# x by channels with two chunks on raw x, host-laid bias tables, attention as three chains, and another order of the output projection

## The chip, the cores and the metric

One NeuronCore of a Trainium2 chip runs the whole program. The time is device microseconds of one execution, the median of several. Engines by the profile's names: PE (TensorE matmuls and transposes), DVE (VectorE), ACT (ScalarE), POOL (GpSimd), SP (SyncE, which issues most DMAs).

## The reference

```python
hn = rms_norm(x, ln_g)                      # x: 1024 tokens x 1024 channels, fp32
proj = hn @ w_in + b_in                     # 3584 columns
glu_a, glu_b, z_conv, q, k, v, z_att = split(proj)          # 512 columns each
y_conv = conformer_conv(glu_a, glu_b, ...)  # GLU, 31 depthwise taps, LayerNorm, silu, pointwise 512x512
y_att = neighbourhood_attention(q, k, v, rpb)  # 8 heads of 64, 16x64 grid, window 8x16, bias per head
y_conv = grouped_rms_norm(y_conv) * silu(z_conv)
y_att  = grouped_rms_norm(y_att)  * silu(z_att)
out = rms_norm(x + concat(y_conv, y_att) @ w_out) * final_g
```

## The kernel before

Every fp32 product is made of three fp32r matmuls, hi·hi, lo·hi and hi·lo: an operand's rounded copy (hi) is made by ACT, what the rounding left (lo) by DVE or POOL as source minus hi. All of `mm` stands on line 127, all transposes on 131, all ACT copies on 136, all DVE work on 140, POOL's on 144; so rows are read by tile names.

A planner in Python writes the order of the five engines when the program is built. `Clock.weave` runs generators ("streams") by rank, lets `Ring`s hand out buffers and PSUM banks, keeps estimated queues for ACT, DVE and POOL, and puts the conv taps (`all_taps`) where DVE's queue is short. The engines then run exactly that order.

- **Head.** Eight 512 KB loads bring x by tokens. Per token tile: squares with a sum (ACT, or DVE for tiles 4 and 6), rsqrt as a power on POOL, x times rsqrt (DVE). 64 PE transposes `px` turn it to channels on partitions; ACT makes hi from the bank (times ln_g), DVE lo. From these 16 tiles `hi0..7`, `lo0..7` (128 channels x 1024 tokens, two halves of 512) all projections are computed.
- **Projections.** w_in goes through in 28 chunks of 128 columns: `pb`, `pa` (GLU), `pq`, `pk`, `pv`, `pz` (gates), each 2 halves x 8 k x 3 matmuls of 512 columns. The raw chunk comes by DMA (`wr`), ACT makes `wh`, POOL `wl` (two subtracts of 128x512 a chunk). LEAD and FILL list the chunks' order. `pv` reads hi and lo in a permuted column order.
- **Convolution.** `glu` on DVE, then 31 taps a channel block on `acc` (DVE, 128x1024 each), then per token tile LayerNorm (transposes `ln`, ACT and DVE, transposes back `lnb`), swish (`th`, `uh`, `ul`), the pointwise matmuls `pw`, group norm, transposes `yt`, copies into `acc`.
- **Attention.** 8 heads x 4 column blocks. Scores `s` on PE, bias and row minimum in one DVE operation, exp on ACT (`prob`), transposes `ptp`, hi (`pth`, ACT) and lo (`ptl`, DVE), then `po`. It is one stream: scores(n+1), transposes(n), products(n). The bias tables with -1e30 outside the window are built by the kernel through DRAM (`rp8`, `ab`, `abn`, `row` DMAs) and loaded by four DMAs a table and head (`load_bias`).
- **Gates and end.** `gated` reads a gate's bank after the normalised output y is there. `final_gates` computes `pz11` and `pz27`, then the output projection: w_out split into `woh`, `wol`, y split into `yh`, `yl` per token tile, 17 groups of 24 matmuls of up to 512 columns, residual, final RMSNorm, store. k order 0, 1, 2, 4, 5, 6, 3, 7 (0 to 3 conv, 4 to 7 attention), tiles 0 and 1 interleaved first.

Of the kernel before, what the change touches and what calls it, by code (L numbers as in the profile page):

```python
# [17 lines left out]
P = 128  # L18
# [9 lines left out]
KH = 8  # L28
TAPS = 31
EPS = 1e-6  # L30
NEG = -1e30

# [7 lines left out]
HF = [(0, 11), (4, 12)]  # L40

LEAD = "g0 g1 g2 q0 k0".split()
FILL = "g3 q1 k1 q2 k2 q3 a0 k3 a1 a2 c0 c1 c2".split()
N_PW = 16
# [5 lines left out]
BV = "pj"  # L50
PEL, PEA, PEB, MMO = 0.3, 0.15, 0.15, 0.0025
# [3 lines left out]
QI = 0.1  # L55
LW = 10.9
SQ_DVE = (4,6)
# [32 lines left out]
class Clock:  # L90
# [58 lines left out]
def block(ctx: ExitStack, tc: tile.TileContext, x, vecs, w_in, dw_w, pw_w, pw_b, rpb, w_out, final_g, out):  # L149
# [16 lines left out]
    r_u, r_raw, r_w, r_x, r_uh, r_ul, r_gz, r_y = ring(16), ring(1), ring(2), ring(XB), ring(1), ring(0), ring(1), ring(1)  # L166
    r_pt, r_os = ring(2), ring(2)
# [20 lines left out]

    x2 = x[0]
# [31 lines left out]
    for t in range(4):  # L221
        xload(t)
    raw0 = wraw(0)
    for t in range(4, NT):
        xload(t)
    land = [4.5, 5.9, 7.4, 8.9, 11.8, 13.3, 14.7, 16.2]
    land_w = LW

    vec = half_tile("uh", "vec")[:V_N, :P]
    nc.scalar.dma_start(out=vec, in_=vecs)  # L230
    dwr = half_tile("ul", "dwr")[:TAPS, :C]
    nc.sync.dma_start(out=dwr, in_=dw_w[0])
# [3 lines left out]
    cols = const.tile([P, V_N], F32, name="cols")  # L236
    pv = bank("tr", "pv")
    nc.tensor.transpose(out=pv[:, :V_N], in_=vec, identity=ident[:V_N, :V_N])
    nc.vector.tensor_copy(out=cols, in_=pv[:, :V_N])
# [4 lines left out]
    dwc = const.tile([P, NC4, 32], F32, name="dwc")  # L244

    def tap_cols():
        yield 19.0
        yield from r_tr.get()
        pd = bank("tr", "pd")
        for c in range(NC4):  # L250
            ck.tp(pd[:, c * 32:c * 32 + TAPS], dwr[:, c * P:(c + 1) * P], ident[:TAPS, :TAPS])
        t = ck.dve("tensor_scalar", out=dwc[:, :, :TAPS],
                   in0=pd[:, :NC4 * 32].rearrange("p (c k) -> p c k", k=32)[:, :, :TAPS], scalar1=0.5, scalar2=None,
                   op0=ALU.mult)
        r_tr.put(t)
        r_ul.put(t)
# [4 lines left out]
    x_ready, hn_ready = {}, {}  # L261

    def x_tile(t):
        yield land[t]
        ss = sm.tile([P, 1], F32, tag="ss", name=f"ss{t}")
        rs = sm.tile([P, 1], F32, tag="rs", name=f"rs{t}")
        eng = "dve" if t in SQ_DVE else "act"
        while t >= 4 and ck.q[eng] > ck.now + QI:
            yield ck.now + 0.1
        if t in SQ_DVE:  # L270
            e = ck.dve("scalar_tensor_tensor", out=acc[:, t % 4, :], in0=xt[t], scalar=1.0 / 1024.0, in1=xt[t],
                       op0=ALU.mult, op1=ALU.mult, accum_out=ss)
        else:
            e = ck.act(out=acc[:, t % 4, :], in_=xt[t], func=AF.Square, scale=1.0 / 32.0, accum_out=ss)
        yield e
        ck.gps("tensor_scalar", 0.2, e, out=rs, in0=ss, scalar1=EPS, scalar2=None, op0=ALU.add)
        e = ck.gps("tensor_tensor", 0.47, 0.0, out=rs, in0=rs, in1=mhalf[:, :1], op=ALU.pow)
        yield e
        x_ready[t] = ck.dve("tensor_scalar", e, 0.55, out=xt[t], in0=xt[t], scalar1=rs, scalar2=None, op0=ALU.mult)

    def turned(h):

        todo_ = list(range(NK))
        for group in ((("tr", "tr", "s", "s", "o", "ln"),) if h == 0 else ()) + (("tr",), ("s",)) * NK:
            ks, todo_ = todo_[:len(group)], todo_[len(group):]
            pts = []
            for k, tag in zip(ks, group):
                yield from RB[tag].get()
                pts.append((k, tag, bank(tag, f"px{h}_{k}", NB[tag])))
            for j in range(4):  # L290
                t = 4 * h + j
                while t not in x_ready:
                    yield ck.now + 0.1
                if x_ready[t] + ck.HOP > ck.now:
                    yield x_ready[t] + ck.HOP
                for k, tag, pt in pts:
                    ck.tp(pt[:, j * P:(j + 1) * P], xt[t][:, k * P:(k + 1) * P], ident)
                    if j == 3:
                        sl = slice(512 * h, 512 * h + 512)
                        e = ck.act(out=hi[k][:, sl], in_=pt, func=AF.Copy, scale=col(V_LN + k))  # L300
                        ck.spawn(low(h, k, pt, sl, e, RB[tag]), -1)
            yield
        for _ in range(4):
            r_u.put()

    def all_turned():
        for h in range(2):
            yield from turned(h)

    def low(h, k, pt, sl, t, r):  # L310
        yield t
        t = ck.dve("scalar_tensor_tensor", t, out=lo[k][:, sl], in0=pt, scalar=col(V_LN + k),
                   in1=hi[k][:, sl].bitcast(F32), op0=ALU.mult, op1=ALU.subtract)
# [12 lines left out]
    ck.q["pool"] = 5.0
# [10 lines left out]
    def prefetch():  # L337
        for n in range(len(order)):
            if n < W_AHEAD or "pw" in state:
                yield from r_raw.get()  # L340
                raw, end = (wraw(n), ck.now + 4.0) if n else (raw0, land_w)
# [7 lines left out]
            for k0 in range(0, NK, KS):  # L349
                kk = slice(k0, k0 + KS)  # L350
                t = ck.act(out=whi[:, kk, :], in_=raw[:, kk, :], func=AF.Copy)
                ck.jobs.append((t, partial(low_weight, n, raw, whi, wlo, kk)))
                yield

    def low_weight(n, raw, whi, wlo, kk):
        k = dict(out=wlo[:, kk, :], in0=raw[:, kk, :], in1=whi[:, kk, :].bitcast(F32), op=ALU.subtract)
        t = ck.gps("tensor_tensor", 0.1 + 0.0022 * KS * P, **k)
        ready.setdefault(n, (whi, wlo, []))[2].extend([t] * KS)
        if kk.stop == NK:
            r_raw.put(t)  # L360
# [875 lines left out]
```

## Time and profile before

| | us |
|---|---|
| median of 3 runs (lowest, highest) | 569.93 (569.51, 573.39) |
| the profiled execution | 572.21 |
| its span, first to last instruction | 570.4 |
| PE busy | 539.3 |
| DVE busy | 412.2 |
| ACT busy | 260.1 |
| POOL busy | 195.1 |

The profiled execution is 1.81 us longer than its span, and 2.28 above the median. Busy times of PE count pipelined matmuls, whose durations overlap; what one matmul adds to the time is read from a run of equal ones.

### The profile page before, as it was taken

The page shows a single profiled execution, that of the slowest core. Times are in us where ns is not written, and L with a number is a line of the kernel's source. Part 1 is how long each engine was busy: PE and PEld are TensorE (multiplying, and loading weights), DVE is VectorE, ACT ScalarE, POOL GpSimd, SP SyncE. Part 2 cuts the span into 40 slices and gives each one's busy share as a digit, 9 for nine tenths or more (in the row PEclk, how much of TensorE's full clock was granted, in tenths as well). Part 3 has the DMA queues.
Part 4 walks back from the last instruction along what each step waited for, and adds up shares of the span by engine and source line. Part 5 has one row for each costly group of instructions (what it writes and reads, how often), then busy time and mean ns, then how long its engine had stood idle before and what let it go on. Part 6 is the DMA issues. An engine that isn't in the chain of part 4 may idle for free.

```text
span 570.4 us, 7827 instructions
## 1 busy us (share of the span) xinstructions
PE 539.3 (95%) x2717; PEld 447.2 (78%) x2717; DVE 412.2 (72%) x665; ACT 260.1 (46%) x634; POOL 195.1 (34%) x176
## 2 busy tenths in 40 slices
PE   4999999898999998999997999999999999999995
PEld 3688888676888886888786788788888888888885
DVE  4747999987999979988999884667564365464232
ACT  6552221124555153655465645875665555253121
POOL 7513543232222343232525152542515552031121
PEclk9999999998999999999998999999999999999999
DMA  9413546663123442263241241101101470044221
GB/s 330 145 14 84 168 128 223 172 192 111 40 57 103 125 105 66 74 149 103 65 142 54 77 120 46 38 26 52 39 0 38 158 284 0 2 148 145 78 75 74
DMA packets 62331, 57.74 MB, mean 101 GB/s; under 512 B 9981, under 2 KB 51765, under 8 KB 62292
## 3 DMA queue, kind: packets, MB, share of 16 engines
q1 hardware_dynamic: 62222, 57.22, 33.6%
q8 instruction: 21, 0.34, 0.3%
q14 instruction: 18, 0.15, 0.1%
q10 hardware_dynamic: 70, 0.03, 0.0%
HBM read 36.58 MB, written 11.58 MB: 84 GB/s over the span
## 4 chain that ended last, share of the span: by engine, by line
PE 71%; DVE 17%; DMA 4%; issue 3%; ACT 2%; SPq 2%; POOL 1%; POOLq 0%; ACTq 0%; DVEq 0%
PE out L127 15%; PE pz L127 13%; DVE acc L140 12%; PE pv L127 6%; PE pk L127 6%; PE pq L127 5%; PE po L127 4%; PE pw L127 4%; PE pb L127 4%; PE ptp L131 3%; PE pa L127 3%; PE s L127 3%; DMA kl<-kl 1%; PE po L131 1%; DMA x<-in_x 1%
## 5 line engine op out<-in xcount | busy, mean ns | idle before, releaser
L140 DVE SCALAR_TENSOR_TENSOR acc<-glu,dwc,acc 128x512 f32<-128x512 f32 (+25 forms) x150 | 186.7, 1270 | 1.2
L144 POOL TENSOR_TENSOR wl<-wr,wh 128x512 fp32r<-128x512 f32 x56 | 93.9, 1695 | 153.0 <-ACT wh L136 147.7
L127 PE MATMUL pz<-hi,wh 128*128 128x512 f32 x128 | 52.2, 408 | 0.0
L127 PE MATMUL out<-wol,yh 128*128 128x512 f32 (+1 forms) x136 | 51.2, 377 | 0.0
L127 PE MATMUL out<-woh,yl 128*128 128x512 f32 (+1 forms) x136 | 51.2, 377 | 0.0
L127 PE MATMUL out<-woh,yh 128*128 128x512 f32 (+1 forms) x136 | 51.2, 377 | 0.0
L127 PE MATMUL pz<-hi,wl 128*128 128x512 f32 x128 | 50.3, 393 | 0.1
L127 PE MATMUL pz<-lo,wh 128*128 128x512 f32 x128 | 50.1, 391 | 0.0
L136 ACT ACTIVATE wh<-wr 128x512 fp32r<-128x512 f32 x56 | 32.3, 628 | 30.5 <-DMA wr<-in_w_in 20.9
L140 DVE TENSOR_TENSOR ptl<-ptp,pth 128x512 fp32r<-128x512 f32 x64 | 37.0, 614 | 1.2 <-ACT pth L136 1.2
L136 ACT ACTIVATE pth<-ptp 128x512 fp32r<-128x512 f32 x64 | 31.8, 543 | 13.2 <-PE ptp L131 12.4
L140 DVE CUSTOM_DVE_ANT_0 s<-s,bias 128x264 f32<-128x264 f32 (+1 forms) x64 | 30.2, 512 | 7.3 <-PE s L127 4.2
L140 DVE TENSOR_TENSOR xr<-out,xr 128x512 f32<-128x512 f32 (+1 forms) x17 | 11.1, 660 | 33.6 <-PE out L127 29.1
L136 ACT ACTIVATE prob<-s,mx 128x264 f32<-128x264 f32 (+1 forms) x64 | 33.6, 536 | 0.6 <-DVE mx L140 0.4
L136 ACT ACTIVATE os<-po 128x256 f32<-128x256 f32 x32 | 12.4, 387 | 41.9 <-PE po L127 41.8
L131 PE MATMUL ptp<-ident,prob 128*128 128x128 f32 x224 | 30.0, 273 | 0.0
L127 PE MATMUL pq<-hi,wh 128*128 128x512 f32 x64 | 26.6, 416 | 3.2 <-DVE v L140 3.2
L127 PE MATMUL po<-pth,v 128*128 128x256 f32 x112 | 29.5, 291 | 0.0
L144 POOL TENSOR_TENSOR ams<-ams,mhalf 128x8 f32<-128x8 f32 x8 | 14.6, 1819 | 43.5 <-DVE ams L140 43.5
L127 PE MATMUL po<-ptl,v 128*128 128x256 f32 x112 | 29.3, 290 | 0.0
L127 PEld LDWEIGHTS out<-woh,yh 128*128 128x128 f32 x136 | 25.6, 188 | 4.7
L127 PEld LDWEIGHTS out<-woh,yl 128*128 128x128 f32 x136 | 25.6, 188 | 4.7
(153 smaller groups left out, 1371.0 us busy)
## 6 DMA issues: line engine op xcount, KB each, us to landing
wr<-in_w_in SPq DMA_DIRECT2D x28, 512.0 KB
x<-in_x SPq DMA_DIRECT2D x8, 512.0 KB
wor<-in_w_out SPq DMA_DIRECT2D x8, 512.0 KB
xr<-in_x SPq DMA_DIRECT2D x8, 512.0 KB
out<-xr SPq DMA_DIRECT2D x16, 256.0 KB
kh<-kh SPq DMA_DIRECT2D x24, 128.0 KB
kl<-kl SPq DMA_DIRECT2D x24, 128.0 KB
q<-ql SPq DMA_DIRECT2D x16, 128.0 KB
```

The source lines that it names most:

```text
L127: self.nc.tensor.matmul(out, lhsT=lhsT, rhs=rhs, start=start, stop=stop)
L131: self.nc.tensor.transpose(out=out, in_=in_, identity=identity)
L136: self.nc.scalar.activation(**k)
L140: getattr(self.nc.vector, fn)(**k)
L144: getattr(self.nc.gpsimd, fn)(**k)
```

## The change

The host now hands over x a second time by channels (`xt`), w_in with each chunk contiguous, taps and vectors as columns, and three finished bias tables; q's weights and bias are scaled by 0.125 in the kernel instead of the scores (their low part is made on DVE).

- **Head.** x comes by channels in 16 half rows of 256 KB. The first two chunks (`RAW`: pb0, pa0) are multiplied with raw x times ln_g, and their results by `rsb` (the rsqrt of each token, on all partitions) afterwards. Per half row: hi copy and square on ACT, lo on DVE, the squares' sum on DVE. `stats`: 4 transposes `sq`, 4 ACT copies with sums, the power on POOL, 4 more transposes that broadcast, one ACT copy. Then `normalise`: xc times ln_g times rsb (DVE), hi again (ACT), lo again on DVE (even k) or POOL (odd k). Only then can the chunks after the second run.
- **Attention.** Three streams: `all_scores`, `turns`, `attention`, with two sets of `prob`. The v transposes `pvt` use the banks o and ln instead of pj; `pv` reads hi and lo in plain order.
- **Gates.** z = (pz + b)(1 + tanh) of the conv gates goes to a kept tile before y is ready (3 DVE operations, before 2). FILL has a0 and a1 earlier; N_PW is 20. The planner's costs for PE and DVE are raised.
- **End.** k order 4 to 7, then 0 to 3. The first group is tiles 0, 1 and 2, its PSUM banks s, s, pj, pj, o, tr. The last two of w_out's splits (k = 2, 3) take tiles that come free after pw7. x is loaded again after all splits.

```diff
+RAW = ((0, 0), (1, 0))
-FILL = "g3 q1 k1 q2 k2 q3 a0 k3 a1 a2 c0 c1 c2".split()
-N_PW = 16
+FILL = "g3 q1 k1 a0 q2 k2 a1 q3 k3 a2 c0 c1 c2".split()
+N_PW = 20
...
+    def x_raw(k, h):
...
+        t = ck.act(out=hi[k][:, sl], in_=xc[k][:, sl], func=AF.Copy, scale=col(V_LN + k))
...
+        t2 = ck.act(out=sq, in_=xc[k][:, sl], func=AF.Square, scale=1.0 / 32.0)
+        yield t
+        raw_ready[k, h] = ck.dve("scalar_tensor_tensor", t, out=lo[k][:, sl], in0=xc[k][:, sl], scalar=col(V_LN + k),
+                                 in1=hi[k][:, sl].bitcast(F32), op0=ALU.mult, op1=ALU.subtract)
+        if k:
+            yield t2
+            t2 = ck.dve("tensor_tensor", t2, out=acc[:, 0, sl], in0=acc[:, 0, sl], in1=sq, op=ALU.add)
...
+    def stats(h):
...
+        for j in range(4):
+            e = ck.act(out=rsb[:, 512 * h + j * P:512 * h + (j + 1) * P], in_=pb[:, j * P:(j + 1) * P], func=AF.Copy,
+                       accum_out=ss[:, j:j + 1])
...
+        e = ck.gps("tensor_tensor", 1.1, 0.0, out=rs, in0=rs, in1=mhalf[:, :4], op=ALU.pow)
...
+    def normalise(h):
...
+        for k in range(NK):
+            t = ck.dve("scalar_tensor_tensor", out=xc[k][:, sl], in0=xc[k][:, sl], scalar=col(V_LN + k), in1=rsb[:, sl],
+                       op0=ALU.mult, op1=ALU.mult)
+            ck.spawn(split_x(k, h, sl, t), -1)
...
+    def split_x(k, h, sl, t):
+        yield t
+        t = ck.act(t, out=hi[k][:, sl], in_=xc[k][:, sl], func=AF.Copy)
+        yield t
+        q = dict(out=lo[k][:, sl], in0=xc[k][:, sl], in1=hi[k][:, sl].bitcast(F32), op=ALU.subtract)
+        t = ck.gps("tensor_tensor", 1.4, t, **q) if k % 2 else ck.dve("tensor_tensor", t, **q)
...
     def load_bias(head, t):
...
+        nc.sync.dma_start(out=bias[t], in_=tabs[t][head])
...
+    def raw_b(j, h, c, uj, sgs, pj, sl, banks):
...
+        t = ck.dve("tensor_tensor", out=sg, in0=pj, in1=rsb[:, sl], op=ALU.mult)
...
-            pvv, sl = yield from proj(wv, h, f"pv{i}_{h}", 8)
...
+            pvv, sl = yield from proj(wv, h, f"pv{i}_{h}")
...
+        if c in zt:
+            z = zt[c][:, sl]
+            t = ck.dve("tensor_scalar", t, 0.5, out=th, in0=th, scalar1=1.0, scalar2=None, op0=ALU.add)
+            t = ck.dve("scalar_tensor_tensor", t, out=z, in0=pz, scalar=col(V_BIN + c), in1=th, op0=ALU.add, op1=ALU.mult)
...
+            t = ck.dve("tensor_tensor", out=y[:, sl], in0=y[:, sl], in1=z, op=ALU.mult)
...
         ck.spawn(attention(), 1)
+        ck.spawn(turns(), 2)
+        ck.spawn(all_scores(), 3)
         ck.spawn(fill(), 5)
...
+    K_OUT = list(range(4, 8)) + list(range(4))
...
-            r = r_u if n < K_BIG else r_hn
+            r = r_hn if n < 6 else r_u
...
-        tags = ("tr", "tr", "s", "s", "o", "ln", "pj", "pj")
+        tags = ("s", "s", "pj", "pj", "o", "tr", "tr", "ln")
...
-        for ts in ((0, 1), (2,), (3,), (4,), (5,), (6,), (7,)):
+        for ts in ((0, 1, 2), (3,), (4,), (5,), (6,), (7,)):
```

The planner's order shows what the diff can't. First DVE in the head. Before, behind the second half's scaling of x stand the eight lo of that half, with the GLU products between them, and then the taps (`acc<-glu`):

```order
L140 SCALAR_TENSOR_TENSOR lo4_143<-px1_4_384,cols_124,hi4_135 128x512
L140 SCALAR_TENSOR_TENSOR lo5_144<-px1_5_390,cols_124,hi5_136 128x512
L140 SCALAR_TENSOR_TENSOR glu0_173<-sg0_0_319,glu0_173 128x512
L140 SCALAR_TENSOR_TENSOR lo6_145<-px1_6_403,cols_124,hi6_137 128x512
L140 SCALAR_TENSOR_TENSOR lo7_146<-px1_7_410,cols_124,hi7_138 128x512
L140 SCALAR_TENSOR_TENSOR glu0_173<-sg0_1_452,glu0_173 128x512
L140 TENSOR_SCALAR acc_99<-glu0_173,dwc_130,cols_124 128x1024
L140 SCALAR_TENSOR_TENSOR acc_99<-glu0_173,dwc_130,acc_99 128x1009
```

After, behind the last sum of squares of the first half (names with xc are x by channels, `sg` and `glu0` are the results of the raw chunks):

```order
L143 SCALAR_TENSOR_TENSOR xc6_106<-xc6_106,cols_108,rsb_156 128x512
L143 SCALAR_TENSOR_TENSOR xc7_107<-xc7_107,cols_108,rsb_156 128x512
L143 TENSOR_TENSOR sg0_0_334<-pb0_0_178,rsb_156 128x512
L143 TENSOR_TENSOR glu0_170<-pa0_0_249,rsb_156 128x512
L143 TENSOR_TENSOR lo0_148<-xc0_100,hi0_140 128x512
L143 TENSOR_TENSOR lo2_150<-xc2_102,hi2_142 128x512
L143 TENSOR_TENSOR lo4_152<-xc4_104,hi4_144 128x512
L143 TENSOR_TENSOR sg0_1_407<-pb0_1_302,rsb_156 128x512
L143 TENSOR_TENSOR lo6_154<-xc6_106,hi6_146 128x512
L143 SCALAR_TENSOR_TENSOR xc0_100<-xc0_100,cols_108,rsb_156 128x512
```

Between the squares and the taps DVE now has sixteen multiplications by rsb, of which half stand in this piece ahead of everything, four multiplications of raw results, and eight subtracts (the other eight are on POOL).

Second, PE at the start of the output projection. Before, the last gate's matmuls are followed by out0 and out1 alone:

```order
L127 MATMUL pz27_1_4563<-hi7_138,wh27_4536 128x512
L127 MATMUL pz27_1_4563<-lo7_146,wh27_4536 128x512
L127 MATMUL pz27_1_4563<-hi7_138,wl27_4537 128x512
L127 MATMUL out0_0_4565<-woh0_4552,yh0_4585 128x512
L127 MATMUL out0_0_4565<-wol0_4553,yh0_4585 128x512
L127 MATMUL out0_0_4565<-woh0_4552,yl0_4586 128x512
L127 MATMUL out0_1_4566<-woh0_4552,yh0_4585 128x512
```

After, the transposes of the last two LayerNorm tiles (`yt6`, `lnb7`) and the pointwise product of the last token tile (`pw7`) stand behind the gates:

```order
L128 MATMUL pz27_1_4181<-hi7_147,wl27_4141 128x512
L134 MATMUL yt6_4453<-ident_94,xn6_4231 128x128 x4
L134 MATMUL lnb7_4469<-ident_94,xn7_4352 128x128 x4
L128 MATMUL out0_0_4442<-woh4_4262,yh0_4271 128x512
L128 MATMUL out0_0_4442<-wol4_4263,yh0_4271 128x512
L128 MATMUL out0_0_4442<-woh4_4262,yl0_4272 128x512
L128 MATMUL out0_1_4465<-woh4_4262,yh0_4271 128x512
L128 MATMUL out0_1_4465<-wol4_4263,yh0_4271 128x512
L128 MATMUL out0_1_4465<-woh4_4262,yl0_4272 128x512
L128 MATMUL pw7_4512<-pwh0_2815,uh7_4495 128x512
```

Of the output projection only out0_0's and out0_1's first k stand between `lnb7` and `pw7`.

Third, ACT at the same place. Before, the w_out splits stand in a row ahead of the first late gate:

```order
L136 ACTIVATE woh5_4672<-wor5_4550 128x1024
L136 ACTIVATE woh6_4689<-wor6_4624 128x1024
L136 ACTIVATE woh3_4705<-wor3_4626 128x1024
L136 ACTIVATE woh7_4721<-wor7_4650 128x1024
L136 ACTIVATE yh2_4725<-acc_99 128x384
L136 ACTIVATE gz11_0_4728<-pz11_0_4560,hcols_128 128x512
```

After, `lnb7` is read by `xn7`, from which `th7` and `uh7` are made, and `uh7` is what `pw7` reads:

```order
L139 ACTIVATE acc_99<-yt6_4453,hcols_135 128x128 x4
L139 ACTIVATE yh1_4449<-ya1_2327 128x128
L139 ACTIVATE gz11_0_4467<-pz11_0_4164,hcols_135 128x512
L139 ACTIVATE xn7_4352<-lnb7_4469,hcols_135 128x128 x4
L139 ACTIVATE th7_4478<-xn7_4352 128x512
L139 ACTIVATE yh1_4449<-ya2_3073 128x128
L139 ACTIVATE gz11_1_4485<-pz11_1_4179,hcols_135 128x512
L139 ACTIVATE yh0_4271<-acc_99 128x128
L139 ACTIVATE yh1_4449<-acc_99 128x128
L139 ACTIVATE yh1_4449<-ya3_4089 128x128
L139 ACTIVATE uh7_4495<-xn7_4352 128x512
L139 ACTIVATE woh2_4526<-wor2_4388 128x1024
```

The gate functions (`gz`) and the splits of y (`yh`) moved in between the LayerNorm's steps, and the last two w_out splits (`woh2`, `woh3`) moved behind `uh7`.

## Rows read from the trace of the kernel before

**Rows 1.** The page: busy us (share of the span) and instructions
```profile
PE 539.3 (95%) x2717; PEld 447.2 (78%) x2717; DVE 412.2 (72%) x665; ACT 260.1 (46%) x634; POOL 195.1 (34%) x176
```

**Rows 2.** Windows: us, busy PE, PEld, DVE, ACT, POOL, PEclk, DMA, GB/s
```profile
0.00:67.10 67.10, 57.90 (x262) 46.34 (x263) 44.10 (x48) 28.20 (x47) 30.72 (x47) 1.00 0.48 144
67.10:139.50 72.40, 66.24 (x282) 52.88 (x282) 67.57 (x62) 17.28 (x35) 26.24 (x16) 0.98 0.58 173
139.50:307.60 168.10, 162.09 (x896) 136.13 (x893) 154.50 (x264) 86.21 (x223) 50.83 (x29) 1.00 0.35 93
307.60:476.60 169.00, 165.72 (x875) 138.71 (x876) 103.89 (x203) 98.44 (x244) 71.74 (x60) 0.99 0.24 74
476.60:564.00 87.40, 87.39 (x409) 73.17 (x407) 40.75 (x88) 28.72 (x84) 14.61 (x24) 1.00 0.23 79
46.80:127.70 80.90, 77.01 (x334) 62.44 (x333) 78.86 (x59) 17.15 (x28) 31.46 (x20) 1.00 0.56 163
```

**Rows 3.** Chain that ended last: start us, us, what
```profile
110.90 4.94 DMA row<-abn
116.44 3.70 DMA kl<-kl
123.71 3.47 DMA kl<-kl
...
476.64 87.36 PE out L127 x408
```

**Rows 4.** The same chain: runs of equal PE pieces
```profile
31.94 0.87 PE px L131 x8
...
39.88 5.45 PE pa L127 x24
...
149.53 0.95 PE po L127 x8
...
194.96 7.30 PE pv L127 x30
...
220.56 3.81 PE pq L127 x15
```

**Rows 5.** Timeline of ACT, 0 to 46: start, us, what, [idle before]
```profile
4.24 1.06 ACT L136 ACTIVATE acc<-x 128x1024 f32<-128x1024 f32 x1 [2.02 <-DMA x<-in_x]
...
12.79 3.57 ACT L136 ACTIVATE hi<-px,cols 128x512 fp32r<-128x512 f32 x6 [0.72 <-PE px L131]
```

**Rows 6.** Timeline of DVE, 0 to 47
```profile
14.36 2.72 DVE L140 SCALAR_TENSOR_TENSOR lo<-px,cols,hi 128x512 fp32r<-128x512 f32 x4
...
46.08 0.69 DVE L140 SCALAR_TENSOR_TENSOR glu<-sg,glu 128x512 f32<-128x512 f32 x1 [9.43 <-ACT glu L136]
```

**Rows 7.** Timeline of POOL, 30 to 60
```profile
41.20 2.54 POOL L144 TENSOR_TENSOR wl<-wr,wh 128x512 fp32r<-128x512 f32 x2 [12.45 <-ACT wh L136]
48.21 4.09 POOL L144 TENSOR_TENSOR wl<-wr,wh 128x512 fp32r<-128x512 f32 x2 [4.47 <-ACT wh L136]
```

**Rows 8.** The chain, 45 to 55: two taps
```profile
47.66 1.28 DVE acc L140
...
48.96 2.19 DVE acc L140
```

**Rows 9.** Timeline of PE, 100 to 136: matmuls with a wait before
```profile
101.17 0.49 PE L127 MATMUL pk<-hi,wh 128*128 128x512 f32 x1 [0.85 <-DVE ql L140]
...
108.55 0.50 PE L127 MATMUL pk<-hi,wh 128*128 128x512 f32 x1 [1.63 <-DVE ql L140]
...
134.55 1.09 PE L131 MATMUL pvt<-ident,vt 128*128 128x128 f32 x4 [0.54 <-DVE v L140]
```

**Rows 10.** Timeline of PE: lnb and the next pw
```profile
425.94 0.60 PE L131 MATMUL lnb<-ident,xn 128*128 128x128 f32 x4
...
434.21 0.39 PE L127 MATMUL pw<-pwh,uh 128*128 128x512 f32 x1
```

**Rows 11.** Lines by form: count | busy us, mean ns | idle
```profile
L136 ACT ACTIVATE woh<-wor 128x1024 fp32r<-128x1024 f32 x8 | 8.4, 1055 | 8.2 <-PE pz L127 8.2
```

More of the change, by code (lines that the diff above doesn't have):

```diff
@@ L243, in block @@
     hcol = lambda r: hcols[:, r:r + 1]
[L244 to L256, printed above, removed]
+    qcols = const.tile([P, 4], F32, name="qcols")
@@ L281, in turned @@
[L281 to L301, printed above, removed]
-            yield
-        for _ in range(4):
-            r_u.put()
@@ L750, in attention @@
                 yield
+            r_p.put(ck.now + PEB)
             for s in pts:
@@ L756, in attention @@
                 r_tr.put(s[5])
+            turned[n] = pts
+    def attention():
+        for n, (i, a, b) in enumerate(blocks):
+            at[0] = n
+            while n not in turned or pair[i][3] is None:
+                yield ck.now + 0.2
+            v, tv = pair[i][3]
+            yield tv
+            head = 2 * i + a
+            if b == 0 and a == 0:
+                yield from r_y.get()
+                ytok = att.tile([P, 8, 2, 64], F32, tag="ytok", bufs=1, name=f"ytok{i}")
+            g0, ng, bt = BLK[b]
             yield from r_o.get()
             po = bank("o", f"po{head}_{b}", 1)
-            for gg, m, ptp, pth, ptl, t in pts:
+            for gg, m, ptp, pth, ptl, t in turned.pop(n):
                 yield t + PEA
@@ L1027, in out_weights @@
             woh[k], wol[k] = (hi_, t), lo_
-    last = {}
-    LATE = (3, 7)
-    K_OUT = [k for k in range(NK) if k not in LATE] + list(LATE)
     def final_gates():
         ends = (CH_ZC + 3, CH_ZA + 3)
+        yield from keep(ends[0])
         pz = {}
-        tags = ("o", "ln", "pj", "pj")
+        tags = ("pj", "pj", "s", "s")
         for n, tag in enumerate(tags):
@@ L1058, in final_gates @@
             yield
-        for h in range(2):
-            for c, tag in zip(ends, (tags[h], tags[2 + h])):
-                y = acc[:, 3, :] if c < CH_Q else ya[3][0]
-                t = yield from gated(y[:, 512 * h:512 * h + 512], pz[c, h], c, h, RB[tag])
-                last[3 if c < CH_Q else 7, h] = t
+        for c, tag in reversed(list(zip(ends, ("pj", "s")))):
+            for h in range(2):
+                ck.spawn(gated(c, h, pz[c, h], RB[tag]), -1)
     def split_y(t):
@@ L1102, in out_tiles @@
             yield from split_y(t)
-    def out_late():
-        for t in range(NT):
-            yield from split_late(t)
     def x_again():
+        while len(woh) < NK:
+            yield ck.now + 0.2
         for t in range(NT):
@@ L1195, in final_rows @@
     def final_rows():
+        while CH_ZC + 3 not in zt and len(ln_end) < NT:
+            yield ck.now + 0.2
         yield from r_u.get()
```

474 lines of the change are left out of this document (258 added, 216 removed).

## The prediction

> **What bounds the kernel now.** I read the page first: PE is busy 539.3 us, 95% of the span, DVE 72%, ACT 46% [rows 1]. So the time is PE's work plus the places where PE stands, and the question is where those places are. Busy PE overstates the work, because a matmul's records overlap; so I price matmuls by runs of equal ones in the chain [rows 4]. A 512-column one costs 5.45/24 = 0.227 us, one of `pq` 0.254, of `pv` 0.243, a 256-column one 0.119, a transpose 0.109; the scores' 128 I put at 0.13 (264 and 288 columns) and 0.17, an estimate by columns. With the counts in each part of the program's order this gives PE's work, and the windows [rows 2] give the length of the same part. The cuts are the last `pa1` (67.1), the first `ptp` (139.5), the first `ln` (307.6), the last gate (476.6) and the last out matmul (564.0):
>
> - to 67.1: work 51.1 (69 transposes, 192 plain matmuls), lost 16.0;
> - to 139.5: work 64.1, lost 8.3;
> - to 307.6: work 161.4, lost 6.7;
> - to 476.6: work 160.8, lost 8.2;
> - to 564.0: work 87.4, lost 0.0 (408 out matmuls without a gap [rows 3]).
>
> Behind the last matmul come 570.4 − 564.0 = 6.4, and 1.8 outside the span. Of 572.2 some 39 are losses. The second part's are waits for the bias tables and for k (the chain runs there over 4.94 of `row<-abn` and 3.70 and 3.47 of `kl` [rows 3]) and for DVE (0.85, 1.63, 0.54 [rows 9]). From 46.8 to 127.7 DVE is busy 78.86 of 80.90 [rows 2]: there the taps are the bound, and every other user of DVE waits in line.
>
> **PE's work after.** 64 transposes `px` go (64 × 0.109 = 7.0 saved), 16 `sq` come (1.7), and `pv` in plain order should fall to the plain price (192 × 0.016 = 3.1 saved, at worst 0). In all 515.9 against 524.8. By the same cuts, in the new order: 45.3, 60.2, 188.4 (gates and attention steps stand ahead of the first `ln` that stood behind it), 131.4, 90.6 (12 matmuls of `pw7`, 4 transposes).
>
> **Head.** The raw stage is paced by ACT: per half row a hi copy, 3.57/6 = 0.60 [rows 5], and a square of 512 columns, 0.57 as half of 1.06 plus a fixed part. Sixteen such pairs are 18.7, four weight copies 2.4, four sum copies some 1.6; the first x tile was there at 4.2 before [rows 5], so ACT is through at about 27, and `rsb` of the first half stands at 27.6. Then DVE has 25 operations up to the first lo of the second half, at 2.72/4 = 0.68 each [rows 6]: 17.0, so 44.6. That is without POOL. Beside them POOL makes seven subtracts, and those are not free for DVE: a pair of `wl` subtracts takes 2.54 alone and 4.09 beside taps [rows 7], and the two taps at that moment take 2.19 instead of 1.28 [rows 8], 0.91 each. A second price is an average: from 46.8 to 127.7 the unslowed DVE work by my count is 48 taps × 1.28, 3 starts × 0.82, 8 × 0.69 = 69.4, and DVE was busy 78.9, so 16 subtracts there cost about 0.6 each. Seven cost 4.2 to 6.4. The first projection on normalised second-half data, `pb1_1`, so starts at 48.8 to 51.0, say 49.9; `pb1_0` fits ahead of it. Three projections of 5.45 follow, and `pa1` ends at 66. Before it was 67.1. **The head gains 1 us**: the 512 KB tiles, the turn and the scaling are replaced by a second pass of 16 multiplications and 16 subtracts. If the subtracts cost nothing it ends at 61, at 1.27 each (all of a subtract's time) at 70.
>
> The Trainium skill, page "SBUF — State Buffer", section "SBUF: two separate sides", says that DVE and POOL share a port pair under an exclusive lock, so that the loser waits in full. The rows above show both slowed instead, 0.91 of the 1.27 on DVE. By the rule seven subtracts would cost 8.9 in place of 5.3, and the head would end 3.6 later.
>
> **First attention.** Table DMAs, v's permuted banks and the wait for `kl` go from PE's path, since the tables come finished and scores run ahead as a chain of their own. The taps start later, at 52 to 55 instead of 46.8 (DVE's `glu` at 46.08 before [rows 6]). Up to the first softmax step the new order has 38 taps instead of 48: 38 × 1.28, twelve shorter ones 8.1, POOL's eleven subtracts 6.6, in all 63, so DVE is there by 118. PE comes there at 66 + 60.2 + 1.4 for short waits = **127.7**, and DVE no longer sets it. Before: 139.5. This is the gain of the change, 12 us, and it is the part I trust most.
>
> **Middle, to the first `ln`.** PE has 188.4 now. DVE's list in this part is 172 at unslowed prices, before 154 (of which the window shows 154.5 busy [rows 2]): 52 long taps instead of 42, 31 short instead of 45, four more attention steps, six q splits from POOL. With the slowing of POOL's subtracts it is about 184, nearly as long as PE's work. I take 5 us of waits (before 6.7 with a looser DVE but one chain), bounds 2 to 12. First `ln` at 127.7 + 188.4 + 5 = 321.1.
>
> **To the last gate.** 131.4, with waits of 4 instead of 8.2 (attention steps are fewer there, and DVE had room: 103.9 busy in 169.0 [rows 2]). Bounds 1 to 9. That gives 456.5.
>
> **End.** Work 90.6. But here the order adds a wait that was not there. Behind `lnb7` PE has only out0_0 and out0_1 with one k, six matmuls, 1.4 us; then `pw7`, which needs `xn7`, `th7`, `uh7` and `ul7`. From `lnb` to its `pw` it took 434.21 − 425.94 = 8.3 in the trace [rows 10], with other work between. So PE stands 6.9, and up to 10 if ACT's gates and y splits between make the chain longer. Everything of the projection is queued behind it. Next, out2 of the first group waits for its split of y, which stands on ACT behind `woh2` and `woh3` (1.06 each [rows 11]), whose tiles come free only after `pw7`: 2.7 more. With 0.5 for a clock that dips after a stall the part loses 10.1, before 0: 456.5 + 90.6 + 10.1 = **557.2**.
>
> Then 6.4 and 1.8 as before: 565.4 against 572.2, a gain of 6.8 by the profiled execution. That one lies 2.3 above the median, so against the median I predict 569.9 − 6.8 = **563**. The sum: head −1.1, first attention −10.7 more, middle +25.3 for 27.0 more work, the last-gate part −33.6 for 29.4 less, end +13.3 for 3.2 more work.
>
> **Rivals.**
>
> *Much faster, 552.* With three chains, the waits in the middle and before the gates all but vanish (5 + 4 become 2 + 1), and the planner's stall before `pw7` is hidden: the chain from `lnb` to `pw` shrinks since nothing is queued on DVE at the end (40.75 busy of 87.4 [rows 2]), leaving 4 of 10. 563 − 6 − 5 = 552. For it: DVE and ACT are loose at the end. Against: 8.3 was measured where DVE was also only 60% busy. Chance 0.19.
>
> *No change, 570.* The gain of the tables is given back: DVE was the bound ahead of the first attention, and the work that it doesn't do there it does later. If each of POOL's subtracts in the middle costs 0.91 rather than 0.6, and a tap late in the line stops `ptl` or `v`, the middle loses 12 instead of 5, which leaves the gain within 1%. The end stall at 10 instead of 6.9 does the same together with a late head. 563 + 7 = 570. For it: 184 of DVE beside 188 of PE is no slack; the waits on DVE in the old trace came when DVE was 97% busy. Chance 0.32.
>
> *Slower, 577.* DVE becomes the bound from the first softmax step to the first LayerNorm. Its list of 172, with 16 weight subtracts and 8 large products of POOL that each cost it 0.91 or more, is 172 + 22 = 194, and with idle of 10 to 15 (it waits for ACT's `pth`, scores and banks as one in-order engine) 204 to 209, against PE's 188. It decides from about 17 over PE's work on, since the kernel gains 12 ahead of it and I already count 5 here. Then 563 + 14 = 577. Against: such idle was 13.6 of 168.1 before [rows 2], and part of that was for PE. Chance 0.10. By the lock that the Trainium skill's page on SBUF describes, all 1.27 of each subtract would fall on DVE, and this case would be nearer.
>
> *It doesn't do what it says:* the tables' DMAs were hidden by the taps anyway (DVE 97% busy), so the first attention comes no earlier than the taps let it: 139.5 − 10 taps of 1.28 + the later start of 7 = 134, and 563 + 6 = 569. This has the same time as no change and I count it there.
>
> **How the numbers follow.** The forecast's own case, 558 to 568, has 0.39, of which 0.30 lies below 564.2. A measurement of this kernel can tell about 1% from no change, which is 564.2 and 575.6. Faster by over 1%: 0.19 from the first rival, 0.30 from the forecast's own; same: 0.09 + 0.30 from own case's top and the second rival; slower: 0.10 and a little of the second. So 0.49, 0.39, 0.12. The range 551 to 576 takes in the first two rivals with the bounds of the head (61 to 70) and middle (2 to 12); outside are the third and the luckiest tail.
>
> **What would show it.** Right: in the profile after, PE's last `pa1` ends near 66, the first `ptp` starts near 128, waits for DMA are gone ahead of it, the first `ln` near 321, and before `pw7` PE stands some 7 us for ACT or DVE with a lower granted clock behind it. The forecast is wrong if DVE is busy over 95% from the first `ptp` to the first `ln` with PE's waits on `ptl` or `v` above 12 us in sum; if `pa1` ends past 70; or if `pw7` follows `lnb7` by less than 4.

## The result: 1.5% slower

The changed kernel takes 579.48 us (median of 4, 578.97 to 580.48), the kernel before beside it 570.88 (4 runs, 569.51 to 573.39): a ratio of 1.0148, 95% interval 1.0106 to 1.0189. I had forecast 563 with a range of 551 to 576. The profiled execution took 579.53 with a span of 577.7.

The page of the kernel after, the line that answers to [rows 1]:

```profile
PE 535.4 (93%) x2664; PEld 443.7 (77%) x2664; DVE 444.3 (77%) x711; ACT 274.4 (47%) x672; POOL 187.8 (33%) x150
```

PE is busy 3.9 us less in a longer span, and DVE 32 us more. The windows of the kernel after, cut at the same events as [rows 2] (last `pa1`, first `ptp`, first `ln`, last gate, last out matmul; columns as there), with three short ones:

```profile
0.00:73.10 73.10, 55.70 (x209) 42.69 (x210) 64.27 (x73) 42.01 (x85) 39.18 (x33) 0.91 0.33 112
73.10:132.60 59.50, 59.50 (x268) 49.02 (x267) 54.06 (x50) 15.99 (x31) 16.07 (x10) 1.00 0.35 98
132.60:326.80 194.20, 189.31 (x1053) 161.56 (x1052) 176.04 (x301) 98.68 (x255) 48.35 (x27) 1.00 0.33 92
326.80:467.50 140.70, 134.67 (x707) 111.66 (x705) 100.86 (x184) 80.73 (x195) 61.28 (x50) 1.00 0.23 75
467.50:571.10 103.60, 96.14 (x433) 78.77 (x432) 47.68 (x104) 35.75 (x104) 21.96 (x30) 0.95 0.22 77
...
50.00:55.00 5.00, 0.77 (x2) 0.50 (x2) 5.00 (x6) 4.06 (x7) 4.22 (x3) 0.77 0.04 16
55.00:60.00 5.00, 5.00 (x14) 3.90 (x13) 4.93 (x6) 0.00 (x0) 2.22 (x2) 0.54 0.34 101
...
475.00:480.00 5.00, 3.41 (x8) 1.82 (x6) 4.27 (x10) 4.88 (x12) 0.00 (x0) 0.50 0.00 0
```

| stretch | before | forecast | after | after minus forecast |
|---|---|---|---|---|
| to the last pa1 | 67.1 | 66 | 73.1 | +7.1 |
| to the first ptp | 72.4 | 61.7 | 59.5 | −2.2 |
| to the first ln | 168.1 | 193.4 | 194.2 | +0.8 |
| to the last gate | 169.0 | 135.4 | 140.7 | +5.3 |
| to the last out matmul | 87.4 | 100.7 | 103.6 | +2.9 |

The five differences make 13.9 of the 16.5 between forecast and result. Nearly all of the rest is the 2.3 that I took off because the profile of the kernel before lay that much above its median; the profile of the kernel after lies on its median.

The first attention and the middle came near the forecast. The longest waits of PE in the kernel after (total us, times, longest):

```profile
PE pb L128 <- DVE lo L143: 6.9, 5, 4.2
PE pb L128 <- ACT wh L139: 6.5, 1, 6.5
PE yt L134 <- POOL xn L148: 4.2, 1, 4.2
PE pb L128 <- POOL wl L148: 3.8, 1, 3.8
```

Three of the four are in the head, one at the end; the 6.5 is only the time until the first weights are there. Against the kernel before, this kernel loses time at both ends and not between.

**The head.** DVE of the kernel after (start, us, what):

```profile
29.50 5.39 DVE L143 SCALAR_TENSOR_TENSOR xc<-xc,cols,rsb 128x512 f32<-128x512 f32 x8 [0.30 <-ACT rsb L139]
...
36.01 1.89 DVE L143 TENSOR_TENSOR lo<-xc,hi 128x512 fp32r<-128x512 f32 x3
37.81 0.69 DVE L143 TENSOR_TENSOR sg<-pb,rsb 128x512 f32<-128x512 f32 x1
38.41 1.20 DVE L143 TENSOR_TENSOR lo<-xc,hi 128x512 fp32r<-128x512 f32 x1
39.53 11.52 DVE L143 SCALAR_TENSOR_TENSOR xc<-xc,cols,rsb 128x512 f32<-128x512 f32 x8
50.97 0.68 DVE L143 TENSOR_TENSOR glu<-pa,rsb 128x512 f32<-128x512 f32 x1
...
52.65 5.72 DVE L143 TENSOR_TENSOR lo<-xc,hi 128x512 fp32r<-128x512 f32 x4
```

The eight multiplications of the first half take 5.39, almost alone, and the eight of the second half 11.52, when POOL works. POOL at that time, the first four subtracts together and then, from narrower windows, the first by itself and two later ones with DVE beside them:

```profile
36.02 8.10 POOL L148 TENSOR_TENSOR lo<-xc,hi 128x512 fp32r<-128x512 f32 x4
44.08 1.71 POOL L148 TENSOR_TENSOR wl<-wr,wh 128x512 fp32r<-128x512 f32 x1
45.76 3.42 POOL L148 TENSOR_TENSOR lo<-xc,hi 128x512 fp32r<-128x512 f32 x2
...
36.02 3.04 POOL L148 TENSOR_TENSOR lo<-xc,hi 128x512 fp32r<-128x512 f32 x1
...
40.72 3.40 POOL L148 TENSOR_TENSOR lo<-xc,hi 128x512 fp32r<-128x512 f32 x2
39.53 5.14 DVE L143 SCALAR_TENSOR_TENSOR xc<-xc,cols,rsb 128x512 f32<-128x512 f32 x3
```

And PE, waiting first for a `wl` that stands on POOL behind four lo, then for the first lo of the second half, and running at half speed behind each wait:

```profile
45.85 0.77 PE L128 MATMUL pb<-hi,wl 128*128 128x512 f32 x1 [3.84 <-POOL wl L148]
...
49.84 0.39 PE L128 MATMUL pb<-hi,wh 128*128 128x512 f32 x1
54.45 0.80 PE L128 MATMUL pb<-lo,wh 128*128 128x512 f32 x1 [4.23 <-DVE lo L143]
...
56.75 0.63 PE L128 MATMUL pb<-hi,wh 128*128 128x512 f32 x1
57.18 0.63 PE L128 MATMUL pb<-lo,wh 128*128 128x512 f32 x1
...
62.17 0.39 PE L128 MATMUL pa<-hi,wh 128*128 128x512 f32 x1
```

From one matmul to the next it is 0.43 at 57 and 0.227 in [rows 4]; the granted clock of the window 55 to 60 is 0.54 (and 0.53 from 45.8 to 49.4), so mostly the lower level, 1.2 GHz, behind a stretch in which PE was busy 0.77 of 5 us.

**The end.** POOL and then PE of the kernel after:

```profile
464.73 2.39 POOL L148 TENSOR_TENSOR wol<-wor,woh 128x1024 fp32r<-128x1024 f32 x1 [5.76 <-ACT woh L139]
467.20 1.08 POOL L148 TENSOR_SCALAR lrs<-mv 128x1 f32<-128x1 f32 x1
468.37 0.57 POOL L148 TENSOR_TENSOR lrs<-lrs,mhalf 128x1 f32<-128x1 f32 x1
468.92 1.64 POOL L148 TENSOR_TENSOR cms<-cms,mhalf 128x8 f32<-128x8 f32 x1
470.63 1.18 POOL L148 TENSOR_TENSOR xn<-xn,cms 128x512 f32<-128x512 f32 x1
```

```profile
471.87 0.66 PE L134 MATMUL yt<-ident,xn 128*128 128x128 f32 x4 [4.18 <-POOL xn L148]
473.75 1.11 PE L134 MATMUL lnb<-ident,xn 128*128 128x128 f32 x4 [1.23 <-ACT acc L139]
...
479.01 0.79 PE L128 MATMUL pw<-pwh,uh 128*128 128x512 f32 x1 [1.59 <-ACT uh L139]
```

The gates end at 467.5. `yt6` waits for a group norm whose steps stand on POOL behind a w_out subtract, `lnb7` behind it in PE's order, `pw7` behind that. The granted clock of the window 475 to 480 is 0.50, the lower level.

### The profile page after: what moved, and what is told of

The parts are those of the page before. It is cut to its first block, busy times and chain, and to the rows that moved or that the text cites. A ratio compares the mean times of both kernels' runs of the same rounds, so it can differ in the third digit from the quotient of the medians.

```text
span 577.7 us, 7567 instructions
## 1 busy us (share of the span) xinstructions
PE 535.4 (93%) x2664; PEld 443.7 (77%) x2664; DVE 444.3 (77%) x711; ACT 274.4 (47%) x672; POOL 187.8 (33%) x150
## 5 line engine op out<-in xcount | busy, mean ns | idle before, releaser
L143 DVE SCALAR_TENSOR_TENSOR acc<-glu,dwc,acc 128x512 f32<-128x512 f32 (+25 forms) x150 | 182.2, 1241 | 0.7
L148 POOL TENSOR_TENSOR wl<-wr,wh 128x512 fp32r<-128x512 f32 x48 | 78.0, 1640 | 181.2 <-ACT wh L139 181.2
L134 PE MATMUL ptp<-ident,prob 128*128 128x128 f32 x224 | 32.9, 273 | 3.3 <-DVE ptl L143 3.3
L128 PE MATMUL pb<-lo,wh 128*128 128x512 f32 x64 | 28.1, 438 | 6.9 <-DVE lo L143 6.9
L128 PE MATMUL pb<-hi,wh 128*128 128x512 f32 x64 | 27.8, 435 | 6.5 <-ACT wh L139 6.5
L128 PE MATMUL pb<-hi,wl 128*128 128x512 f32 x64 | 27.8, 434 | 4.0 <-POOL wl L148 3.8
L134 PEld LDWEIGHTS ptp<-ident,prob 128*128 128x128 f32 x224 | 26.0, 140 | 5.8 <-issue 2.5
```

The costliest lines, as they stand in the source:

```text
L134: self.nc.tensor.transpose(out=out, in_=in_, identity=identity)
```

## The experiments

Times are medians, ratios are to the kernel before run beside them, with their 95% interval. "End" is the stretch behind the last gate.

**All second lo on DVE.**

```diff
-        t = ck.gps("tensor_tensor", 1.4, t, **q) if k % 2 else ck.dve("tensor_tensor", t, **q)
+        t = ck.dve("tensor_tensor", t, **q)
```

> The kernel after, with all sixteen second lo of x on DVE instead of eight of them on POOL; everything else as the planner then orders it. Theory A (the head is late because DVE's multiplications by rsb take 1.44 us each beside POOL's subtracts instead of 0.67): eight more DVE operations of 0.65 cost 5.2, but 8 x 0.77 and 4 x 0.75 of slowing go, so the last pa1 ends at about 70 instead of 73.1 and the time falls 2 to 5 us. Rival B (the sheer number of DVE operations in the second pass sets it, not POOL): pa1 ends at 76 to 78 and the time rises 3 to 5 us.

579.61, ratio 1.0133 (1.0110 to 1.0156): no gain, though the head did what theory A says. DVE, the first and last windows, then three waits of PE:

```profile
40.93 5.38 DVE L143 SCALAR_TENSOR_TENSOR xc<-xc,cols,rsb 128x512 f32<-128x512 f32 x8
```

```profile
0.00:68.90 68.90, 54.66 (x208) 41.60 (x209) 60.00 (x81) 41.12 (x85) 28.47 (x25) 0.90 0.37 126
...
461.90:571.00 109.10, 98.87 (x429) 80.00 (x428) 48.28 (x103) 35.90 (x102) 18.46 (x27) 0.92 0.21 73
```

```profile
466.34 0.79 PE L128 MATMUL pw<-pwh,uh 128*128 128x512 f32 x1 [3.73 <-ACT uh L139]
...
475.47 0.47 PE L128 MATMUL out<-woh,yh 128*128 128x512 f32 x1 [1.94 <-DVE z L143]
...
480.43 1.11 PE L134 MATMUL yt<-ident,xn 128*128 128x128 f32 x4 [3.62 <-POOL xn L148]
```

The multiplications are back at 0.67 each, pa1 ends 4.2 earlier, the last gate 5.6 earlier, and the end is 5.5 longer: the same steps of the last token tiles, in another order, hold PE up there. The end gave it back.

**No raw chunks.** `RAW = ()`, and the raw hi and lo are not made.

> The kernel after without the two chunks on raw x: x comes by channels, is squared and summed, then scaled once, and all chunks use the scaled x. 16 hi copies and 16 lo of raw x and four multiplications of raw results are gone. Theory A (two passes over x are what makes the head 6 us later than before): PE starts near 19 instead of 6.5, but the second half is ready near 40, pa1 ends at 63 to 66 instead of 73.1, and the time falls 7 to 10 us. Rival B (the raw chunks do fill PE's wait and the loss comes from the granted clock at 46 to 62 alone): pa1 ends at 70 to 74, and the time is the same within 3 us.

588.73, ratio 1.0285 (1.0256 to 1.0313). Both theories missed: pa1 ended at 83.7. PE's first projection started at 32.7, since the planner put the second half's transposes of sums (`sq`) ahead of it, and these waited 12.4 for DVE. So this run doesn't price the raw chunks. With x by channels no token's `rsb` can be there before all channels are summed, and without the raw chunks PE has no projection to begin until then.

**pw7 later, w_out's lows on DVE, two tiles first.**

```diff
-            t = split(raw, hi_, lo_, land, "dve" if n % 2 else "pool")
+            t = split(raw, hi_, lo_, land, "dve")
...
-        yield e + PEL
+        yield e + (8.0 if t == NT - 1 else PEL)
...
-        for ts in ((0, 1, 2), (3,), (4,), (5,), (6,), (7,)):
+        for ts in ((0, 1), (2,), (3,), (4,), (5,), (6,), (7,)):
```

> The kernel after with its end changed in three places: the low parts of w_out all on DVE, first output group of tiles 0 and 1 instead of 0 to 2, and the planner told to put pw7 later, so that 12 gate and 15 out matmuls stand between lnb7 and pw7 (after: six out matmuls). Theory A (the 13 us lost behind the last gate are yt6 waiting for POOL, whose queue has a w_out subtract in it, then pw7's chain, all at half the clock): the part from the last gate to the last out matmul falls from 103.6 to 92 to 96, the time falls 6 to 10 us. Rival B (the loss is the chain of the last token tiles, which ends as late in any order, so that the waits only move to later out matmuls): the time falls less than 3 us.

581.62, ratio 1.0153 (1.0116 to 1.0190): rival B. The end is 101.4; `yt6` now waits longer, and two out matmuls wait for `z`:

```profile
474.39 1.11 PE L134 MATMUL yt<-ident,xn 128*128 128x128 f32 x4 [6.09 <-ACT uh L139]
```

A w_out low now stands ahead of the group norm's sums on DVE, at 469.43, where it waits 3.59 for ACT; POOL's last step for `yt6` ends at 474.33.

**One chain for attention.** `all_scores`, `turns` and `attention` in one stream.

> The kernel after with attention as one stream again: scores(n+1), transposes(n), products(n). Theory A (the tables from the host and the loads ahead made the first attention 9 us earlier, the three chains add little): the first ptp stays at 131 to 134, the stretch to the first ln grows by 1 to 4, time +0 to +4. Rival B (the three chains make the gain): the first ptp still near 133, but the waits of the middle rise by 8 or more, time +8. Rival C (the chains crowd DVE and cost time): the time falls 2 or more.

589.01, ratio 1.0297 (1.0271 to 1.0323). It looked like rival B, but the middle was shorter (191.6 against 194.2); what grew was the head (75.1 against 73.1) and the gates' stretch:

```profile
326.40:477.50 151.10, 144.00 (x750) 119.64 (x748) 103.92 (x192) 87.42 (x212) 64.65 (x53) 0.98 0.24 76
```

With 750 PE instructions instead of 707 this stretch holds work that stood in the middle and in the end before, `pw7`'s 12 matmuls among it; without them the end still takes 104.1. The run is taken up again below.

**The head of the kernel before** (x by tokens) in the kernel after.

> The kernel after with the head of the kernel before: x by tokens, squares, scaling and the 64 turns by PE, no chunks on raw x; host tables, three chains, gates and end stay those of after. Theory A (the head's second pass puts 20 us of work on DVE, the taps start 12 us later and end 76 us later, at 417 instead of 342, and with them the last token tiles' LayerNorm, pw7 and so the stall at the end): pa1 at 67, last tap at 340 to 375, first ln at 310 to 318, the part behind the last gate at most 95, time 561 to 568, that is faster than both kernels. Rival B (three chains and kept gates give DVE its late taps, the head has little to do with it): pa1 at 67 but the last tap past 395, the end part still above 100, time 570 to 575.

574.05, ratio 1.0056 (1.0025 to 1.0088). The head ends at 68.1, the last tap at 370 instead of 417, pw7 is through at 444, before the gates. Theory A's chain of causes is right to there, and 5 us come back, though its 561 to 568 was missed. But the end is 100.9. PE there:

```profile
468.34 0.50 PE L131 MATMUL out<-woh,yh 128*128 128x512 f32 x1 [3.43 <-DVE ya L146]
470.65 0.79 PE L131 MATMUL out<-woh,yh 128*128 128x512 f32 x1 [1.30 <-DVE ya L146]
474.12 0.77 PE L131 MATMUL out<-woh,yh 128*128 128x512 f32 x1 [1.83 <-ACT yh L142]
478.03 0.80 PE L131 MATMUL out<-woh,yh 128*128 128x512 f32 x1 [2.29 <-DVE z L146]
```

With the late chain gone, other waits stand in its place: out0 and out1 start in the banks s, s, pj, pj, which hold pz27 and pz11 until DVE has read them. Three of the four waits are for that, the third is for a split of y.

**Taps first.** `TQ = 0.6` instead of 0.1 in the kernel after.

> The kernel after with the planner's look-ahead for taps at 0.6 us instead of 0.1 (TQ): a tap is put on DVE's queue while up to 0.6 us of work is in it, so taps come earlier and attention's DVE steps wait longer behind them. Theory A (late taps make the stall at the end): last tap before 395 instead of 417, end part 95 to 98 instead of 103.4, but the middle loses 3 to 8 by waits on ptl and v; time within 4 us of the kernel after. Rival B (DVE is full either way, taps can't come earlier): last tap above 410 and the time the same or worse by the middle's waits.

588.44, ratio 1.0294 (1.0241 to 1.0347). The last tap ended at 318, 100 us earlier, and pw7 before the gates. The stretches to the first ln grew by 7, and the end, 101.4, had the same four waits as the run before (3.43, 1.35, 1.83, 2.29). So late taps are not all that makes the end long: without them the waits for the banks stand there.

**The tables alone**, as far as they can be had alone: the kernel before with host tables and q scaled in its weights.

> The kernel before with the three bias tables from the host (one DMA a table and head) and q scaled by 0.125 in its weights, low parts of q's weights on DVE; nothing else of the change. Theory A (the waits for tables and k's copies ahead of the first attention go): first ptp at 131 to 135 instead of 139.3, time 4 to 7 us below before. Rival B (the tables' DMAs were hidden, since DVE with its taps is 97% busy there): first ptp at 138 to 140, time within 2 us of before.

567.65, ratio 0.9919 (0.9882 to 0.9955): 4.6 us by the ratio, 3.1 by the two medians. The first ptp comes at 131.8, as theory A says. The stretch from pa1 to it:

```profile
66.80:131.80 65.00, 64.08 (x282) 51.70 (x281) 64.86 (x62) 17.20 (x35) 20.80 (x10) 1.00 0.34 89
```

72.4 became 65.0, with DVE full (64.86 busy); 3.6 of it went back in the gates' stretch (172.6).

**Banks.** In the kernel after the first line; with before's head the second, and with two tiles too.

```diff
-        tags = ("s", "s", "pj", "pj", "o", "tr", "tr", "ln")
+        tags = ("tr", "tr", "o", "s", "s", "pj", "pj", "ln")
...
+        tags = ("tr", "tr", "o", "ln", "s", "s", "pj", "pj")
```

> The kernel after with one line changed: the output projection takes its PSUM banks in the order tr, tr, o, s, s, pj, pj, ln, so that its first three tiles' halves don't start in the four banks (pj, pj, s, s) that hold the last gates' results until DVE has read them. Theory A (the first out matmuls wait for these banks, and the wait lowers the clock): the part behind the last gate falls from 103.4 to 95 to 99, the waits of out for z and ya go, time 4 to 8 us less than the kernel after. Rival B (in this kernel the late chain of the last token tile, lnb7 to pw7, sets that part, whatever the banks are): the part stays above 101, time within 2 us of the kernel after.

> The kernel after with the head of the kernel before (as in the earlier run) and the output projection's banks in the order tr, tr, o, ln, s, s, pj, pj: four banks that the last gates don't use come first. Here pw7 is done 20 us before the last gate, so no late chain is left. Theory A: the part behind the last gate falls from 100.9 to 88 to 91, time 560 to 564, faster than both kernels. Rival B (the splits of y and of w_out that ACT and DVE have to do at that point are what PE waits for, not banks): the part stays at 97 or more, time 570 to 574.

> The same with the first output group of two tiles instead of three, as in the kernel before, so that only the four free banks are used first. Theory A: no difference from the run with three tiles that can be told, within 2 us, at 560 to 564. Rival B (with three tiles the third's banks s, s or its split of y, which stands behind the last w_out splits, holds PE up): 2 to 5 us faster than three tiles. Rival C (two tiles use up the ready data sooner and wait for the gated y3): 2 to 4 us slower.

In the kernel after: 579.93, ratio 1.0146 (1.0107 to 1.0185), nothing, rival B. With before's head: 567.86, ratio 0.9936 (0.9917 to 0.9954), and with two tiles 568.03, 0.9947 (0.9919 to 0.9975), so two or three tiles are the same. The end is 95.3 and 94.7, between theory and rival. One wait of over 0.3 us is left behind the last gate (three tiles):

```profile
472.58 0.79 PE L131 MATMUL out<-woh,yh 128*128 128x512 f32 x1 [4.03 <-ACT yh L142]
```

`split_y` does tile 0's k = 7 before it begins tile 1, and k = 7 waits for the last gate.

**That split apart, then the old k order.**

```diff
-        for j in range(4):
+        ck.spawn(split_part(t, yh, yl, slice(7, 8), ya[3][0][:, tsl]), 0)
+        for j in range(3):
...
-    K_OUT = list(range(4, 8)) + list(range(4))
+    K_OUT = [0, 1, 2, 4, 5, 6, 3, 7]
```

> The run with two tiles and four free banks, and one more change: a token tile's split for k = 7 (which waits for the last gate) is a stream of its own, so that the next tile's splits no longer stand behind it on ACT. Theory A (the 4.03 us that out1 waited for yh on ACT, and the lower clock behind it, are this order): the part behind the last gate falls from 94.6 to 88 to 91, time 3 to 6 us less, 562 to 565. Rival B (the wait moves to k = 7, fourth in the order, whose gated y comes from DVE): the part stays above 93, time within 2 us.

> The same with the k order of the kernel before (0, 1, 2, 4, 5, 6, 3, 7), so that both parts that wait for the last gates come last. Theory A: the part behind the last gate is 87.4 to 89, as in the kernel before, time 560 to 564, the lowest of all. Rival B (k order doesn't matter once the splits stand apart): within 1 us of the run before it.

562.78, ratio 0.9839 (0.9803 to 0.9876), and 559.79, 0.9792 (0.9759 to 0.9825). The end of the second, and of the kernel after with its own head and the same four edits (banks as in the first line above):

```profile
463.90:551.20 87.30, 87.30 (x409) 73.27 (x407) 43.99 (x91) 30.82 (x86) 18.39 (x25) 1.00 0.23 79
```

```profile
468.10:562.50 94.40, 92.06 (x433) 76.49 (x431) 47.52 (x100) 36.33 (x101) 24.64 (x31) 1.00 0.24 84
```

> The kernel after with its own head (raw chunks, x by channels) and four changes at the end: banks tr, tr, o, s, s, pj, pj, ln; first group of two tiles; the split for k = 7 as a stream of its own; k order 0, 1, 2, 4, 5, 6, 3, 7. yt6, lnb7 and pw7 then stand between out matmuls. Theory A (head costs 5 to 6, the end's order the rest, and a late lnb7 to pw7 is harmless once out matmuls cover it): the part behind the last gate falls from 103.4 to 91 to 94 (90.6 of it work), time 565 to 570. Rival B (the late chain still sets it, since the splits of w_out for the last k wait for pw7's tiles): the part stays above 97, time 573 or more.

571.86, ratio 1.0016 (0.9993 to 1.0039): the end falls by 9.2, with pw7's 2.7 of work in it, and the clock there is 1.00. The time is slightly above theory A's 570. Beside the 559.79 kernel, which has the head of the kernel before and, but for the order of the banks behind the first three, this end, it is 12 us slower: 5.9 in the head (73.9 and 68.0) and 7.1 in the end (94.4 and 87.3). So with the end repaired the new head costs twice what the stretch to pa1 shows, since it pushes the last token tiles' steps behind the gates: `pw7` and 12 transposes are 4.0 of work there by [rows 4], and PE waits 1.5 for `yt6`.

**One chain, again,** in the 559.79 kernel.

> The best kernel so far (head of before, new end) with attention as one stream. Theory A (three chains are worth waits in the middle): the stretches from the first ptp to the last gate, 336.4 in sum, grow by 5 to 10, time 565 to 570. Rival B (one chain lost its 9 us in the first comparison to the late end and the head's order): within 2 us of the best, 558 to 562.

556.96, ratio 0.9741 (0.9698 to 0.9783): 2.8 us below three chains, which neither theory had; the two intervals overlap, so what is sure is that three chains gain nothing here. Its two middle stretches are 189.2 and 146.3 against 194.3 and 142.1. This is the best kernel of the study.

**All second lo on DVE, with the new end.**

> The kernel after with the new end (as in the run with its own head) and all sixteen second lo of x on DVE. Theory A (POOL's subtracts slow DVE in the head by 4 us, and the end had eaten the gain): pa1 ends at 69 to 70, the part behind the last gate is 90 to 94, time 564 to 568, that is 4 to 7 us below the same without the edit (571.9). Rival B (the end depends on something that the earlier head doesn't move): pa1 at 69 to 70 but the time 570 to 573 as without it.

566.37, ratio 0.9926 (0.9900 to 0.9951): the edit that gave nothing before now gives 0.9%, 5 us. That is theory A's time, with the end at 95.5 instead of its 90 to 94.

## Why the prediction was wrong

**The step that failed first is the head**, "The head gains 1 us". It loses 6, and one of the signs of being wrong that I named came with it: `pa1` ended past 70. My pieces, against the rows: `rsb` stood at 29.5 and not 27.6 (+1.9); from there to the start of the first lo of the second half it took 23.2 and not 22.3 (+0.9), with the subtracts dearer than I put them; PE needs that lo's end, which beside POOL came 1.8 after its start, and I had counted to the start (+1.8); and behind the wait 23 matmuls of `pb1_1` took 7.7 instead of 5.2, about half of them at the lower clock (+2.5). I counted a clock dip at the end and none in the head, though the same kind of gap stood there. That the new head as a whole costs this is shown: with before's head `pa1` ends 5 earlier and the kernel gains 0.9%, or 12 us once the end is repaired. That POOL's subtracts in the second pass make 4.2 of it is shown by the run with them on DVE. How the rest divides between the second pass and the raw chunks stays open, since the run without raw chunks lost its time to another order.

Of POOL's subtracts: in the second eight multiplications the excess is 11.52 − 5.39 = 6.1 us, beside some six POOL subtracts, 1.0 each, where I took 0.6 to 0.91. What the Trainium skill says (page "SBUF — State Buffer", section "SBUF: two separate sides": an exclusive lock, whoever starts first holds it for the whole instruction, and the loser waits in full) is nearer to this than my prices. By that rule either engine can lose, where I had taken DVE to lose each time, and the trace agrees: at 36.01 DVE began first, three of its subtracts ran at their full pace, 0.63, and POOL's first took 3.04, ending 1.2 behind them, so there the loser was POOL. Afterwards the two took turns, and a pair took 1.7, somewhat less than 0.67 and 1.27 in sum.

**The end** was the right step with the wrong size and partly the wrong reason. I had 10.1 lost; it was 13.0. The wait of `pw7` behind `lnb7` was there, but `lnb` to `pw` took 5.3 and not 8.3; in its place `yt6` waited 4.2 for POOL. The wait for y2 didn't show. The waits (4.2, 1.2, 1.6, 0.3) make 7.3. The lower clock makes about 4 by my estimate, where I had put 0.5: from 471.9 to 483.0 the granted clock is 0.54, and eight transposes and 14 matmuls, worth 4.1 at the prices of [rows 4], fill 11.1 with 2.8 of waits. Another 0.9 are eight transposes (`yt6`, `yt7`) that I had not counted.

What I didn't see at all were the layers under it: the last gates' banks, and tile 1's splits behind tile 0's last one. That the banks are hidden by the late token tiles is shown: free banks alone gave nothing in the kernel after, and with before's head they took 5.6 off the end. The split and the k order were only tried on top of them. Three runs on the kernel after (banks; `pw7`, w_out's lows and the first group; lo on DVE) gained nothing. Banks, first group, split and k order together took 1.3%, and lo on DVE on top of these 0.9%.

**The gates' stretch** I forecast with 4 of waits; by the same count it lost 9.3 (before: 8.2). Nine waits of 0.2 to 1.3 make 6.0 of that, seven of them for DVE; the rest doesn't show as waits. Nothing excluded that, and my reason to halve the old number (fewer attention steps, room on DVE) was not enough.

**The first attention** held: 59.5 without a wait, 12.9 less than before, of which the tables and q's scaling alone give 7.4. The other 5.5 are for the most part less work in the stretch and not a shorter wait: PE has 268 instructions there instead of 282, with 12 matmuls of `pb` now behind the first `ptp` (2.7), and the 48 of `pv` are 0.227 apart instead of 0.25 (1.2). The chains don't give it, since it is 59.7 with one.

**The three chains**, named in the much faster rival as what would clear the middle, gain nothing once the end is repaired and before's head is back. (The sum of that rival also slips: a stall that shrinks from 10 to 4 gives 6 and not 5, so 551.) Why one chain cost 1.5% in the kernel after is not shown beyond the stretches given above. The slower rival had the right sign and nearly the time (577), by another mechanism, so that is luck: DVE wasn't the bound of the middle, which came as forecast.

In sum PE's work fell by 8.9 by my count, the first attention lost 9 less, the head lost 12 more and the end 13 more.

## What to carry to other kernels

A gain ahead of a serial tail is only seen when the tail lets it through: test an edit again after the tail is repaired before calling it useless. When results wait in PSUM banks for a last elementwise step, start the next matmuls in other banks and put the operands that depend on that step last. A first pass on raw data that has to be redone later is paid by the engine that redoes it, by the clock of the matmuls that wait for it, and by the later steps that it pushes to the end of the program.

## What was unexpected in the hardware

Beside POOL's subtracts it was not the kind of operation that set DVE's price. Plain subtracts kept 0.63 at 36.01, where POOL's took 3.04, and at 52.65 four of them took 5.72, most about 1.7 each, like the multiplications at 39.53. Where both had work from 38.4 on, DVE's operations with two operands in SBUF and POOL's subtracts (1.7 each, alone 1.27) went in turn, one for one. DVE's operations with one operand in a PSUM bank (`sg` at 37.81, `glu` at 50.97) kept 0.69 and 0.68 beside the same POOL work. And a gap of 4.2 us in PE's work, in a stretch that was already thin, was followed by some 5 us at the lower clock, with matmuls 0.43 apart.
